# A decoder layer on one core: side-chain transfers issued by POOL, weights alone by SP, convolution taps on shifted ranges

## The chip, the cores and the metric

The kernel runs on 1 core of one Trainium2 chip. Times are microseconds (us) on the device, from the profiler or from a timed execution; single operations are also given in nanoseconds (ns). The engines are PE (TensorE matmul; PEld is its weight load), DVE (VectorE), ACT (ScalarE), POOL (GpSimd) and SP (SyncE). Each executes its own instructions in program order; semaphores order them against each other. A DMA is issued by an instruction on SP or on POOL and moved by the core's 16 DMA engines. The metric is the device time of one execution, given as a median of 3.

## The reference, cut to what matters

One layer for 256 prompt positions and 8 sample positions (264 columns together, `T` in the kernel):

```python
p = x @ w_in                      # [u | v_a | q,k,v | z | beta | a | gate_a | gate_b]
y_a = gelu(u) * (tril(W_s[g]) @ LN(gelu(v_a)) + b_s[g])       # 16 groups, chunks of 128
qkv = silu(causal depthwise conv, width 4, of q,k,v)
q, k = l2norm(q) * 128**-0.5, l2norm(k)
beta, g = sigmoid(.), -exp(A_log) * softplus(a + dt_bias)
S_t = exp(g_t) (I - beta_t k_t k_t^T) S_{t-1} + beta_t k_t v_t^T ;  o_t = S_t^T q_t   # 16 heads
y_b = rmsnorm_head(o) * w_onorm * silu(z)
m = (sigmoid(gate_a) * (y_a W_pa) + sigmoid(gate_b) * (y_b W_pb)) W_o
x1 = LN(ALPHA*x + m);  y = LN(ALPHA*x1 + relu(x1 W_up)^2 W_down)
```

The convolution of the prompt starts from zeros, that of the samples from a state that is passed in. Besides y, the last rows before the convolution and the new recurrent states are returned. All weights are float32; D_MODEL is 2048, d_ff 8192, 16 heads of 128.

## The kernel before

**The stream.** All weights pass through PE once, as 305 blocks of 2048 x 128, each in two halves j of 128 x 1024. A half is loaded into one of 4 `raw` buffers (`dma_w`, line 314), rounded by ACT to `hi` (`hi_w`, line 321), and DVE forms `lo = raw - hi` (`lo_w`, line 327). PE then does 24 matmuls of 264 columns per half (`mms`, lines 379 to 381): hi x xh, hi x xl, lo x xh. The order of the blocks is: beta/a; q, k, v of head groups 0 and 1; va; group 2; gate a; group 3; gate b; u; z; then the projections pa, pb, wo; then up and down. In slot j of the main loop (line 1545) PE's half j is written out, then `hi` of half j+4, `lo` of half j+3, the evacuation of the block that has just ended (`evac_...`), up to one step of each side chain (`step`, line 409), and last the load of half j+7.

**Side chains.** Everything else is written as generators, one step at a time, between the slots: `norm_chain` and `delta_chain`, `final_chain`, `out_chain` of each head group g (names n, d, f, o), `lnv_chain`, `sample_chain`, `ya_chain`, `yb_chain`, `x1_chain`, `state_chain`. A step is written out when the program's own estimate (`clk`, `rdy`, `est`, `dma`) says that its data are there. `require` forces a chain to its end where the stream needs its result: o0 before group 3, lnv before u, ya before pa, yb before pb, x1, state. Side chains repack data through DRAM: a store, then a load in another layout (`repack`, line 785; `d_n` to `N`; `d_t` to `W`; `d_r` to `X`), with broadcast loads among them.

**Issuers.** `dma("y", ...)` issues on SP: the weights, and all loads of the chains and most of their stores. `dma("g", ...)` issues on POOL: the stores `d_sga`, `d_sg`, `d_ya`, `d_z`, `d_mac`, `d_o`, `d_r` and a few small ones. A weight load waits on SP for the `lo` that last read its buffer, and what is issued later on SP waits behind it. POOL's other work is the mask of the decay matrix (line 686), the mask of W_s (`load_ws`, line 1168), the copy of the last columns before the convolution (line 1136), and memsets.

**Steps that are named below.** `delta_chain` loads four broadcast tiles `N` and then a tile of identities, `eye`, on which DVE's triangular solve works (lines 728 to 751). `evac_pa` multiplies a gate tile `mc`, which `load_mc` (line 1194) fetched at the start of the block, by the block's result and stores it to `d_mac`. `load_ws` loads a W_s tile, masks it on POOL and loads a bias tile. `yb_chain` (line 973) builds the input of pb in eight pairs of heads; for the last two it waits for o3, and after them it waits for the sample chain and does the sample columns `zs`. `evac_qkv` (line 1114) copies a block to `cv` behind three zero columns and adds three taps with DVE. The small tiles of all evacuations share one pool `e` of 8 buffers.

Of the kernel before, what the change touches and what calls it, by code (L numbers as in the profile page):

```python
# [89 lines left out]
def hybrid_step(ctx: ExitStack, tc: tile.TileContext, I, O):  # L90
# [61 lines left out]
    clk = {"p": 0.0, "v": 0.0, "a": 0.0, "y": 0.0, "g": 0.0, "d": 0.0}  # L152
# [19 lines left out]
    def dma(q, out, in_, track=True, after=0.0):  # L172
        t = max(clk[q], after, rdy.get(in_.tensor.name, 0.0))
        clk[q] = t + (1050.0 if q == "g" else 60.0)
# [6 lines left out]
        (G_ if q == "g" else nc.sync).dma_start(out=out, in_=in_)  # L181
# [404 lines left out]
    def norm_chain(g):  # L586
# [6 lines left out]
        dma("y", out=sc, in_=I["sconv"][:, :, hs, :, :])  # L593
# [48 lines left out]
        dma("y", out=X, in_=d_r[g, 4:8, :].partition_broadcast(P))  # L642
# [4 lines left out]
        dma("y", out=X, in_=d_r[g, 0:4, :].partition_broadcast(P))  # L647
# [9 lines left out]
    def delta_chain(g):  # L657
# [9 lines left out]
        for c in range(2):  # L667
            dma("y", out=D[c], in_=d_gc[hs, c * P:(c + 1) * P].partition_broadcast(P))
        bN = sm("bN", (P, 32))
        for c in range(2):  # L670
            dma("y", out=bN[64 * c:64 * c + 64, :],
# [37 lines left out]
        for c in range(2):  # L709
            dma("y", out=d_p[g, c], in_=Pm[c])  # L710
# [5 lines left out]
        dma("y", out=nd.rearrange("c h a j i -> (a j) c h i"), in_=dg)  # L716
# [7 lines left out]
        dma("y", out=qd, in_=d_eg[hs, P:2 * P].partition_broadcast(P))  # L724
# [10 lines left out]
        dma("y", out=Tt, in_=I["eye"])  # L735
# [21 lines left out]
        for c in range(2):  # L757
            dma("y", out=tdd[c].rearrange("k p i -> p k i"), in_=Tt[64 * c:64 * c + 64])
# [11 lines left out]
    def load_blocks(g, c):  # L770
        W = dt_("W", (P, 4, P))
        dma("y", out=W[:, 0:3, :], in_=d_p[g, c, 0:96].rearrange("(b j) h i -> (j h) b i", b=3))
        dma("y", out=W[:, 3, :], in_=d_t[g, c].rearrange("k (q h a) i -> (k q h) (a i)", q=4, h=HG))
# [11 lines left out]
    def repack(t, src, to_blocks, dst):  # L785
        if to_blocks:
            dma("y", out=t, in_=src)
        else:
            dma("y", out=t.rearrange("(a i) h v -> (i h) a v", a=4), in_=src)
        yield  # L790
        yield
        if to_blocks:
            dma("y", out=dst, in_=t.rearrange("(a i) h v -> (i h) a v", a=4))
        else:
            dma("y", out=dst, in_=t)
# [104 lines left out]
    def load_state(i, pool, bufs):  # L900
        t = pool.tile([P, SK, P], F32, tag="s", bufs=bufs, name=nm("Ss"))
        dma("y", out=t, in_=I["ssm"][:, SK * i:SK * i + SK, :], track=False)
# [787 lines left out]
```

## Time and profile before

| | us |
|---|---|
| median of 3 executions | 1898.2 (1897.77 to 1898.55) |
| the profiled execution, timed | 1898.92 |
| its span in the profile | 1897.2 |
| PE busy in the span | 1884.2 |
| DVE, ACT, POOL busy | 1281.0, 1038.6, 108.2 |

The granted TensorE clock is full but for the first and the last stretch. A row of the windows view gives the busy time of each engine in a stretch of the span; what PE lacks to the length of the stretch is PE's idle time. Waits are listed by the instruction that waited and by what it waited for. In a timeline the square bracket holds the engine's idle time before the instruction, and what ended it.

### The profile page before, as it was taken

What the parts mean: (1) busy time and instruction counts of PE and PEld (TensorE: products, weight loads), DVE (VectorE), ACT (ScalarE), POOL (GpSimd) and SP (SyncE); (2) the same over time, 40 slices, a digit from 0 to 9 for tenths busy, and PEclk for the clock granted to TensorE, in tenths of its full rate; (3) what the DMA queues carried; (4) which work ended last, traced back from release to release, by engine and by line L of the source; (5) the groups of instructions that cost most, each with busy time, mean ns of one, the idle gap of its engine ahead of it and who ended that gap; (6) DMA issues with size and microseconds to landing.
All of it is one profiled execution on the core that took longest, in us unless ns stands there. A gap on an engine that the chain in (4) does not pass through costs nothing.

```text
span 1897.2 us, 38788 instructions
## 1 busy us (share of the span) xinstructions
PE 1884.2 (99%) x15502; PEld 1880.6 (99%) x15502; DVE 1281.0 (68%) x2208; ACT 1038.6 (55%) x1626; POOL 108.2 (6%) x239
## 2 busy tenths in 40 slices
PE   9999999999999999999999999999999999999998
PEld 9999999999999999999999999999999999999998
DVE  6876768857685779877566778756665644444575
ACT  6777466666665544545444557744654455345552
POOL 1110000011111111001000000000000000000000
PEclk9999999999999999999999999999999999999999
DMA  7656575666667877988877655577777755565552
GB/s 237 192 182 213 178 221 188 211 205 220 200 199 242 258 244 246 300 260 285 259 227 229 203 192 180 174 244 244 239 239 245 235 182 182 182 202 180 177 182 98
DMA packets 167684, 406.72 MB, mean 214 GB/s; under 512 B 31184, under 2 KB 67184, under 8 KB 167360
## 3 DMA queue, kind: packets, MB, share of 16 engines
q1 hardware_dynamic: 161856, 388.38, 64.5%
q0 software_dynamic: 5648, 15.87, 2.2%
q8 instruction: 121, 1.98, 0.4%
q14 instruction: 59, 0.48, 0.1%
HBM read 372.96 MB, written 31.62 MB: 213 GB/s over the span
## 4 chain that ended last, share of the span: by engine, by line
PE 85%; DVE 2%; issue 1%; DMA 1%; ACT 0%; DVEq 0%; POOL 0%; SPq 0%; POOLq 0%; ACTq 0%
PE mm L380 27%; PE mm L379 27%; PE mm L381 27%; PE ax L236 3%; DVE lo L216 1%; PE ax L240 1%; DMA raw<-in_wt 0%; DVE G L216 0%; PE st L236 0%; DVE tmp L216 0%; DVE Y L227 0%; DMA G<-d_y 0%; DVE rr L231 0%; DMA d_ya<-gu 0%; DVE N L216 0%
## 5 line engine op out<-in xcount | busy, mean ns | idle before, releaser
L216 DVE TENSOR_TENSOR lo<-raw,hi 128x1024 fp32r<-128x1024 f32 (+1 forms) x614 | 741.8, 1212 | 347.8 <-PE mm L381 166.6
L197 ACT ACTIVATE hi<-raw 128x1024 fp32r<-128x1024 f32 (+1 forms) x614 | 638.8, 1047 | 376.4 <-PE mm L380 248.4
L379 PE MATMUL mm<-xh,hi 128*128 128x264 f32 x1872 | 538.0, 287 | 0.0
L381 PE MATMUL mm<-xh,lo 128*128 128x264 f32 x1872 | 531.2, 284 | 2.6 <-DVE lo L216 2.5
L380 PE MATMUL mm<-xl,hi 128*128 128x264 f32 x1872 | 532.8, 285 | 0.0
L381 PEld LDWEIGHTS mm<-xh,lo 128*128 128x128 f32 x1872 | 352.1, 188 | 3.7 <-DVE lo L216 3.7
L379 PEld LDWEIGHTS mm<-xh,hi 128*128 128x128 f32 x1872 | 353.0, 189 | 0.1
L380 PEld LDWEIGHTS mm<-xl,hi 128*128 128x128 f32 x1872 | 352.0, 188 | 0.1
L380 PE MATMUL mm<-hl,hi 128*128 128x264 f32 x1024 | 291.6, 285 | 0.0
L381 PE MATMUL mm<-hh,lo 128*128 128x264 f32 x1024 | 290.3, 284 | 0.0
L379 PE MATMUL mm<-hh,hi 128*128 128x264 f32 x1024 | 290.1, 283 | 0.0
L379 PE MATMUL mm<-x1h,hi 128*128 128x264 f32 x784 | 223.5, 285 | 0.0
L381 PE MATMUL mm<-x1h,lo 128*128 128x264 f32 x784 | 222.6, 284 | 0.0
L380 PE MATMUL mm<-x1l,hi 128*128 128x264 f32 x784 | 222.3, 284 | 0.0
L379 PEld LDWEIGHTS mm<-hh,hi 128*128 128x128 f32 x1024 | 192.9, 188 | 0.0
L381 PEld LDWEIGHTS mm<-hh,lo 128*128 128x128 f32 x1024 | 192.8, 188 | 0.0
L380 PEld LDWEIGHTS mm<-hl,hi 128*128 128x128 f32 x1024 | 192.2, 188 | 0.0
L380 PEld LDWEIGHTS mm<-x1l,hi 128*128 128x128 f32 x784 | 147.7, 188 | 0.0
L379 PEld LDWEIGHTS mm<-x1h,hi 128*128 128x128 f32 x784 | 147.4, 188 | 0.0
L381 PEld LDWEIGHTS mm<-x1h,lo 128*128 128x128 f32 x784 | 147.2, 188 | 0.0
L216 DVE TENSOR_TENSOR r<-r,mm 128x264 f32<-128x264 f32 x64 | 27.5, 429 | 104.0 <-PE mm L381 104.0
L227 DVE SCALAR_TENSOR_TENSOR ac<-cv,cols,ac 128x256 f32<-128x256 f32 x144 | 69.5, 483 | 7.8 <-ACT ac L197 4.4
(324 smaller groups left out, 3039.5 us busy)
## 6 DMA issues: line engine op xcount, KB each, us to landing
raw<-in_wt SPq DMA_DIRECT2D x602, 512.0 KB
Ss<-in_ssm SPq DMA_DIRECT2D x64, 256.0 KB
out_ssm_s<-Ss SPq DMA_DIRECT2D x32, 256.0 KB
G<-d_r SPq DMA_DIRECT2D x8, 528.0 KB
raw<-in_wt SPq DMA_DIRECT2D x12, 256.0 KB
d_y<-G SPq DMA_DIRECT2D x12, 256.0 KB
G<-d_y SPq DMA_DIRECT2D x12, 256.0 KB
d_sga<-sg POOLq DMA_DIRECT2D x16, 132.0 KB, 4.1
```

What stands on the lines that cost most here:

```text
L197: S.activation(out=out, in_=in_, func=func, scale=scale)
L216: V.tensor_tensor(out=out, in0=a, in1=b, op=op)
L227: V.scalar_tensor_tensor(out=out, in0=a, scalar=s, in1=b, op0=op0, op1=op1)
L236: PE.matmul(out=out, lhsT=lhsT, rhs=rhs, start=start, stop=stop)
L240: PE.transpose(out, in_, idt)
L379: PE.matmul(out=ps, lhsT=hi[:, kk, :], rhs=xh[:, k, :], start=(k == 0), stop=False)
L380: PE.matmul(out=ps, lhsT=hi[:, kk, :], rhs=xl[:, k, :], start=False, stop=False)
L381: PE.matmul(out=ps, lhsT=lo[:, kk, :], rhs=xh[:, k, :], start=False, stop=(k == 15))
```

## The change

- The queue letter "w" is new and stands for SP; only the weight loads, the first loads of the program and the last stores (`out_y`, `out_ys`) carry it. Every other `dma` call becomes "g", that is POOL.
- The program's estimate of an issue on POOL becomes 600 ns instead of 1050. With it and with the separate queues, the estimated times differ, and so the slots in which side-chain steps are written out.
- `evac_qkv` drops the three zero columns of `cv` and their memset; each tap adds the columns that exist into the columns of `ac` that it reaches.
- `yb_chain` waits for the sample chain and does the sample columns before it waits for o3, instead of after the last pair.

```diff
-    clk = {"p": 0.0, "v": 0.0, "a": 0.0, "y": 0.0, "g": 0.0, "d": 0.0}
+    clk = {"p": 0.0, "v": 0.0, "a": 0.0, "w": 0.0, "g": 0.0, "d": 0.0}
...
     def dma(q, out, in_, track=True, after=0.0):
         t = max(clk[q], after, rdy.get(in_.tensor.name, 0.0))
-        clk[q] = t + (1050.0 if q == "g" else 60.0)
+        clk[q] = t + (60.0 if q == "w" else 600.0)
...
-        (G_ if q == "g" else nc.sync).dma_start(out=out, in_=in_)
+        (nc.sync if q == "w" else G_).dma_start(out=out, in_=in_)
...
-        dma("y", out=raw[j], in_=I["wt"][b - 1, :, 8 * h:8 * h + 8, :], after=lo_end.get(j - RAW, 0.0))
+        dma("w", out=raw[j], in_=I["wt"][b - 1, :, 8 * h:8 * h + 8, :], after=lo_end.get(j - RAW, 0.0))
...
-                dma("y", out=N[s][64 * c:64 * c + 64], in_=ndf.unsqueeze(0).to_broadcast([4, 16, 16, 32]))
+                dma("g", out=N[s][64 * c:64 * c + 64], in_=ndf.unsqueeze(0).to_broadcast([4, 16, 16, 32]))
...
-        dma("y", out=Tt, in_=I["eye"])
+        dma("g", out=Tt, in_=I["eye"])
...
         if to_blocks:
-            dma("y", out=t, in_=src)
+            dma("g", out=t, in_=src)
         else:
-            dma("y", out=t.rearrange("(a i) h v -> (i h) a v", a=4), in_=src)
+            dma("g", out=t.rearrange("(a i) h v -> (i h) a v", a=4), in_=src)
...
                 if i == 6:
+                    yield from wait_for("samp")
+                    zs = qt("zs", (P, KT, TS))
+                    dma("g", out=zs, in_=d_z[:, :, TP:T].rearrange("m p b -> p m b"))
+                    yield
+                    yield
+                    stt(zs, VS, col(C_ON, 0), zs, ALU.mult, ALU.mult)
+                    act(hi[:, :, TP:T], zs, AF.Copy)
+                    yield
+                    tt(lo[:, :, TP:T], zs, hi[:, :, TP:T].bitcast(F32), ALU.subtract)
+                    yield
                     yield from wait_for("o3")
...
-        yield from wait_for("samp")
-        zs = qt("zs", (P, KT, TS))
-        dma("y", out=zs, in_=d_z[:, :, TP:T].rearrange("m p b -> p m b"))
...
-        cv = et("cv", (P, 3 + T))
-        G_.memset(cv[:, 0:3], 0.0)
+        cv = et("cv", (P, T))
         cb = 4 * (16 * s + m)
-        act(cv[:, 3:3 + T], ps, AF.Copy)
+        act(cv, ps, AF.Copy)
...
-            stt(ac, cv[:, t:t + TP], col(cb, t), ac, ALU.mult, ALU.add)
-        G_.tensor_copy(out=tail[:, s, j, :], in_=cv[:, 3 + TP - 3:3 + T])
+            stt(ac[:, 3 - t:TP], cv[:, 0:TP - 3 + t], col(cb, t), ac[:, 3 - t:TP], ALU.mult, ALU.add)
+        G_.tensor_copy(out=tail[:, s, j, :], in_=cv[:, TP - 3:T])
...
         w = et("ws", (P, 2, P))
-        dma("y", out=w, in_=I["wst"][:, 2 * i:2 * i + 2, :])
+        dma("g", out=w, in_=I["wst"][:, 2 * i:2 * i + 2, :])
         G_.affine_select(out=w, in_=w, pattern=[[0, 2], [1, P]], base=0, channel_multiplier=-1,
                          compare_op=ALU.is_ge, fill=0.0)
         bs = et("bs", (P, 2, P))
-        dma("y", out=bs, in_=I["b_s"][2 * i:2 * i + 2, :].partition_broadcast(P))
+        dma("g", out=bs, in_=I["b_s"][2 * i:2 * i + 2, :].partition_broadcast(P))
...
         if kind == "pa":
-            dma("y", out=t[0], in_=d_sga[m])
+            dma("g", out=t[0], in_=d_sga[m])
...
-            dma("y", out=O["y"][c * P:c * P + P, s_], in_=y)
+            dma("w", out=O["y"][c * P:c * P + P, s_], in_=y)
```

## Rows read from the trace of the kernel before

**Rows 1.** The page, part 1: busy time of PE and PEld.

```profile
PE 1884.2 (99%) x15502; PEld 1880.6 (99%) x15502; DVE 1281.0 (68%) x2208; ACT 1038.6 (55%) x1626; POOL 108.2 (6%) x239
```

**Rows 2.** The windows view: stretch, then each engine's busy us (instructions).

```profile
0.00:50.00 50.00, 46.92 (x355) 46.19 (x356) 29.49 (x46) 35.06 (x56) 5.72 (x24) 0.97 0.70 233
200.00:250.00 50.00, 47.45 (x384) 46.57 (x383) 40.57 (x96) 19.62 (x28) 0.54 (x1) 1.00 0.61 192
500.00:550.00 50.00, 48.52 (x405) 48.33 (x404) 35.67 (x77) 29.35 (x69) 5.70 (x13) 1.00 0.60 182
1100.00:1150.00 50.00, 49.67 (x405) 49.33 (x404) 39.14 (x63) 27.92 (x47) 0.00 (x0) 1.00 0.57 183
1850.00:1900.00 50.00, 41.64 (x341) 40.94 (x339) 26.54 (x51) 12.20 (x24) 0.00 (x0) 0.97 0.28 91
```

**Rows 3.** Waits of PE: total us, times, longest us.

```profile
PE mm L381 <- DVE lo L216: 2.5, 3, 1.7
PE ax L236 <- DMA G<-d_y: 1.5, 1, 1.5
```

**Rows 4.** Timeline of DVE around three of its waits: start us, us, instruction, wait.

```profile
206.30 0.43 DVE L216 TENSOR_TENSOR G<-G,bN 128x256 f32<-128x256 f32 x1 [7.17 <-issue]
...
527.31 0.43 DVE L216 TENSOR_TENSOR G<-G,bN 128x256 f32<-128x256 f32 x1 [4.95 <-DMA G<-in_eye]
...
711.62 0.23 DVE L216 TENSOR_TENSOR tmp<-N,G 128x72 f32<-128x72 f32 x1 [3.60 <-DMA d_ya<-gu]
```

**Rows 5.** Timeline of SP before those waits, and around the late load d_y.

```profile
192.87 2.21 SPq L181 DMA_DIRECT2D N<-d_n  x4
...
199.17 0.33 SPq L181 DMA_DIRECT2D G<-in_eye  x1
...
525.17 0.38 SPq L181 DMA_DIRECT2D d_y<-G  x1
...
530.52 0.38 SPq L181 DMA_DIRECT2D G<-d_y  x1
```

**Rows 6.** Waits of SP: the largest group.

```profile
SPq L181 <- DVE lo L216: 976.1, 439, 7.6
```

**Rows 7.** DMA issues by line: issuer, count, KB each, median us to landing.

```profile
Ss<-in_ssm SPq DMA_DIRECT2D x64, 256.0 KB
...
d_sga<-sg POOLq DMA_DIRECT2D x16, 132.0 KB, 4.1
...
d_o<-G POOLq DMA_DIRECT2D x8, 256.0 KB, 5.5
...
zs<-d_z SPq DMA_DIRECT2D x1, 64.0 KB
```

**Rows 8.** The tile d_mac: from issue on POOL to landing.

```profile
DMA to landing us min/median/max: 2.3/4.1/6.7
```

**Rows 9.** Groups of POOL by line: two issues, busy us, mean ns.

```profile
L181 POOL DMA_DIRECT2D d_ya<-gu x16 | 8.8, 548 | 44.3 <-issue 13.3 <-DVE ACC L227 11.6 <-DVE G L216 10.1
...
L181 POOL DMA_DIRECT2D out_tails<-tail x4 | 3.0, 745 | 0.3 <-POOL tail L1136 0.3
```

**Rows 10.** Timelines of DVE, POOL and SP in the pa stage.

```profile
874.16 0.43 DVE L216 TENSOR_TENSOR mc<-mm,mc 128x264 f32<-128x264 f32 x1 [1.69 <-PE mm L381]
...
879.93 0.43 DVE L216 TENSOR_TENSOR mc<-mm,mc 128x264 f32<-128x264 f32 x1 [0.23 <-PE mm L381]
...
880.66 0.54 POOL L181 DMA_DIRECT2D d_mac<-mc  x1 [5.23 <-DVE rr L231]
...
880.17 0.38 SPq L181 DMA_DIRECT2D mc<-d_sga  x1
```

**Rows 11.** The zero columns of the convolution, groups of POOL by line.

```profile
L1128 POOL MEMSET cv<- 128x3 f32 x48 | 4.8, 99 | 0.0
```

**Rows 12.** Timelines of DVE and PE: end of yb, start of pb.

```profile
940.93 0.29 DVE L216 TENSOR_TENSOR ybl<-zs,ybh 128x128 fp32r<-128x128 f32 x1
...
944.82 0.29 PE L379 MATMUL mm<-ybh,hi 128*128 128x264 f32 x1
```

More of the change, by code (lines that the diff above doesn't have):

```diff
@@ L641, in norm_chain @@
         yield
-        dma("y", out=X, in_=d_r[g, 4:8, :].partition_broadcast(P))
+        dma("g", out=X, in_=d_r[g, 4:8, :].partition_broadcast(P))
         yield
@@ L709, in delta_chain @@
         for c in range(2):
-            dma("y", out=d_p[g, c], in_=Pm[c])
+            dma("g", out=d_p[g, c], in_=Pm[c])
             for a in range(4):
@@ L715, in delta_chain @@
         yield
-        dma("y", out=nd.rearrange("c h a j i -> (a j) c h i"), in_=dg)
+        dma("g", out=nd.rearrange("c h a j i -> (a j) c h i"), in_=dg)
         for h in range(HG):
@@ L723, in delta_chain @@
         axf()
-        dma("y", out=qd, in_=d_eg[hs, P:2 * P].partition_broadcast(P))
+        dma("g", out=qd, in_=d_eg[hs, P:2 * P].partition_broadcast(P))
         yield
@@ L792, in repack @@
         if to_blocks:
-            dma("y", out=dst, in_=t.rearrange("(a i) h v -> (i h) a v", a=4))
+            dma("g", out=dst, in_=t.rearrange("(a i) h v -> (i h) a v", a=4))
         else:
-            dma("y", out=dst, in_=t)
+            dma("g", out=dst, in_=t)
         yield
@@ L963, in ya_chain @@
                 t[i] = qt("yld", (P, 2, T))
-                dma("y", out=t[i], in_=d_ya[2 * i:2 * i + 2].rearrange("m p t -> p m t"))
+                dma("g", out=t[i], in_=d_ya[2 * i:2 * i + 2].rearrange("m p t -> p m t"))
             if i >= 2:
@@ L982, in yb_chain @@
                 if i == 6:
+                    yield from wait_for("samp")
[8 more added lines that the diff above has]
+                    yield
                     yield from wait_for("o3")
                 t[i] = (qt("yo", (P, 2, TP)), qt("yz", (P, 2, TP)))
-                dma("y", out=t[i][0], in_=d_o[2 * i:2 * i + 2].rearrange("m p t -> p m t"))
-                dma("y", out=t[i][1], in_=d_z[2 * i:2 * i + 2, :, 0:TP].rearrange("m p t -> p m t"))
+                dma("g", out=t[i][0], in_=d_o[2 * i:2 * i + 2].rearrange("m p t -> p m t"))
+                dma("g", out=t[i][1], in_=d_z[2 * i:2 * i + 2, :, 0:TP].rearrange("m p t -> p m t"))
             if 1 <= i < 9:
@@ L1017, in state_chain @@
             yield "wait"
-            dma("y", out=O["ssm_s"][:, SK * i:SK * i + SK, :], in_=s)
+            dma("g", out=O["ssm_s"][:, SK * i:SK * i + SK, :], in_=s)
             if i + 2 < n:
@@ L1196, in load_mc @@
         if kind == "pa":
-            dma("y", out=t[0], in_=d_sga[m])
+            dma("g", out=t[0], in_=d_sga[m])
         else:
-            dma("y", out=t[0], in_=d_mac[m])
+            dma("g", out=t[0], in_=d_mac[m])
             t.append(et("sgb"))
-            dma("y", out=t[1], in_=d_sg[m])
+            dma("g", out=t[1], in_=d_sg[m])
         ten.setdefault("mc", {})[m] = t
@@ L1223, in evac_wo @@
             nx = et("xr")
-            dma("y", out=nx, in_=I["xt"][:, m + 1, :])
+            dma("g", out=nx, in_=I["xt"][:, m + 1, :])
             ten["xr"][m + 1] = nx
@@ L1447, in load @@
                 sl = slice(*part[1:])
-                dma("y", out=wbr[:, sl, :], in_=I["wba"][:, sl, :])
+                dma("w", out=wbr[:, sl, :], in_=I["wba"][:, sl, :])
             elif part[0] == "x":
                 sl = slice(*part[1:])
-                dma("y", out=xs[:, sl, :], in_=I["xt"][:, sl, :])
+                dma("w", out=xs[:, sl, :], in_=I["xt"][:, sl, :])
             elif part[0] == "w":
@@ L1457, in load @@
                     raw[j] = rawp.tile([P, 8, P], F32, tag="raw", name="raw%d" % j)
-                dma("y", out=raw[j][:, lo:hi, :], in_=I["wt"][b - 1, :, 8 * h + lo:8 * h + hi, :])
+                dma("w", out=raw[j][:, lo:hi, :], in_=I["wt"][b - 1, :, 8 * h + lo:8 * h + hi, :])
             else:
-                dma("y", out=rows2, in_=I["rows2"])
-                dma("y", out=cst, in_=I["cst"])
-                dma("y", out=cols, in_=I["cols"])
+                dma("w", out=rows2, in_=I["rows2"])
+                dma("w", out=cst, in_=I["cst"])
+                dma("w", out=cols, in_=I["cols"])
         def split(part):
@@ L1564, in hybrid_step @@
                     xr = et("xr")
[L1565 removed]
+                    dma("g", out=xr, in_=I["xt"][:, 0, :])
                     ten["xr"] = {0: xr}
```

26 lines of the change are left out of this document (9 added, 17 removed).

## The prediction

> **What bounds the kernel now.** I read the busy times first, then the windows, then the waits of PE, and last the timelines of the engines behind each of those waits. PE is busy for 1884.2 of the 1897.2 us [rows 1], with a granted clock of 1.00 wherever the stream is running [rows 2]. The change leaves every matmul in place, so the most that it can give is PE's idle time, 13.0 us. The windows say where that lies [rows 2]: 50 - 46.92 = 3.08 us in the first stretch, 2.55 in 200 to 250, 1.48 in 500 to 550, 0.33 in 1100 to 1150, and 47.22 - 41.64 = 5.58 in the last (the span ends at 1897.22). These sum to 13.0. The first stretch waits for the first weights and the last for the final layer norm; neither is edited. The one at 1100 is the first layer norm. So 2.55 + 1.48 = 4.03 us can go.
>
> The waits of PE name them [rows 3]: three waits for `lo`, 2.5 us together, and one of 1.5 us for a repacked tile `d_y`. Behind the first lies DVE. It sat idle for 7.17 us before the first operation on the identity tile [rows 4], which SP issued at 199.17 [rows 5]; from issue to use that is 7.13 us. While DVE stood, no `lo` was made and the weights in hand were used up. The same load made DVE wait 4.95 us at 527, and a buffer still held by the store `d_ya` cost it 3.60 us at 711 [rows 4]; neither is followed by a wait of PE for `lo` of its own size in the list [rows 3]. I conclude that PE is covered for about 5 us of one DVE wait, and pays for what lies beyond: 7.17 cost 2.5.
>
> **The change part by part.** My sum is made against the profiled execution, 1898.92 us timed, which is 1.7 above its span and 0.7 above the median of 1898.2. I carry differences over to the median.
>
> *Issues moved from SP to POOL.* The list of DMA issues, from `Ss` with 64 to `zs` with 1 [rows 7], has 313 issues of SP that are neither weights, first loads nor last stores. On POOL an issue takes 0.55 us for a plain tile and 0.75 us for one of many short pieces [rows 9], so 313 cost 170 to 235 us of POOL, whose total becomes some 280 to 340 us of 1897. That much of an engine at 6% lies beside PE; the price is latency, not throughput.
>
> *What SP is rid of.* SP waits 976.1 us for `lo` in 439 waits, 2.2 us each, 7.6 at most [rows 6]; these are weight loads waiting for their buffer, and chain transfers stood behind them. In turn, weight loads no longer stand behind a chain's transfer that waits for its data. `d_y` shows it: its store was issued at 525.17, but its load only at 530.52 [rows 5]. POOL has a head of its line too: stores that wait for an evacuation, the copy of the last columns, the masks. Each holds up a chain by up to a slot, so I take no gain in the length of chains, only in latency.
>
> *The identity tile.* From issue to landing POOL's transfers show 4.1 us at 132 KB and 5.5 at 256 KB [rows 7], 2.3 to 6.7 at the extremes [rows 8]. These are stores; for a load of this kind on POOL the trace has no row, and I take them as bounds. In place of 7.13, the 128 KB tile then arrives in 4.1 to 5.5 us, being nearest to the 132 KB rows, and DVE waits about 4.1 to 5.5 us instead of 7.17. The first of these is covered, the second is 0.5 over the 5 us where 2.2 over cost 2.5. So 2.0 to 2.55 us come back; I take 2.2. With 6.7 it would be 0.6.
>
> *The repacked tile.* On POOL the store lands at 525.17 + 4.1 to 5.5 = 529.3 to 530.7 and the load as much later, 533.4 to 536.2. PE waited until 534.63 or so with a wait of 1.5, that is, it came at about 533.1 [rows 3, 5]. So it would wait 0.3 to 3.1 us instead of 1.5: a gain of 1.2 to a loss of 1.6. I take 0.
>
> *New waits on POOL.* Two loops arise. In `load_ws` the mask waits for the landing of a load that POOL has just issued, and the bias load and the next `d_ya` store stand behind it; a late `d_ya` is what held DVE for 3.60 us at 711 [rows 4]. In the pa stage the store of block m (which waits for DVE's product) now stands ahead of the load of `mc` for block m+1, on which DVE's next product waits. Before, SP issued that load beside the store, at 880.17 against 880.66 [rows 10]. The loop is 0.73 us from product to store [rows 10], 0.54 for the store's issue, then the load's landing of 4.1: 5.4 us against a block's 5.77 us, the distance of two products [rows 10]. At 4.1 us it costs nothing. For both loops together I take 1.0 us, within 0 (the loop fits) and 10 (below).
>
> *The weights' own transfers.* A weight load that shared SP's line now shares only the DMA engines with POOL's transfers, and the bytes stay the same. I take 0, between no gain beyond the 4.03 us above and, at worst, one more stall like the one after 200 us, 2.5.
>
> *Convolution.* 48 memsets of 99 ns [rows 11] go from POOL, and each tap loses one to three of 256 columns on DVE. POOL and DVE are not what PE waits for in those stages: 0.
>
> *Sample columns earlier.* The last write of yb's input ends at 941.2, and PE starts pb at 944.8 [rows 12]: 3.6 us to spare, so no gain today. The move shortens the tail after o3 and is the cover if chains on POOL become later. 0.
>
> Sum: -2.2 + 0 + 1.0 + 0 = -1.2 us, 1898.2 - 1.2 = 1897.0.
>
> One rule speaks against the change as such. The Trainium skill says in "DMA: Bandwidth & Descriptors", section "Issuing engines are not separate DMA queues", that issuing from several engines saves only the sequencer's time to start a transfer. By it the result would be the time before; here the trace agrees with the saving it concedes, since SP's line is held by waits, and differs in that these waits are long [rows 6]. Another, in "SBUF — State Buffer", the box on DVE blocking DMA, has POOL's descriptors wait while DVE holds the shared port, with some 3.1 us in place of 0.62. The trace does not show it at this kernel's DVE operations: issues average 548 ns [rows 9].
>
> **The rivals.**
>
> *All of the idle time goes.* If landings on POOL stay near 4.1 us and neither loop costs anything, both stalls go: 1898.2 - 4.03 = 1894.2. For it: DVE's wait at 200 is half queueing, and SP's weights flow freely. Against it: the repack took two landings in series, and only the shortest of POOL's makes it.
>
> *The loop of the pa stage sets the pace, and the kernel is slower.* If a load lands as late as `d_o` did, 5.5 us [rows 7], the loop is 0.73 + 0.54 + 5.5 = 6.8 us, 1.0 over the block. Over 15 blocks that is 15 us, of which about 5 are covered as above: +10, with the -1.2 some 1907. It begins at a landing of 4.5 us (5.77 - 1.27) and is slower by the bound below from (5 + 1.2 + 3.8)/15 = 0.67 over, at 5.2 us. At 6.7 us [rows 8] it would be 1898.2 + 33 - 5 = 1926, which no median in the rows suggests. For it: POOL's order is fixed, and chain transfers of yb and o3 are issued in the same stretch. Against it: the 132 KB median is 4.1.
>
> *It does not do what it says.* POOL's line takes the place of SP's, chains are held as long as before, the waits of DVE move to other places: 1898.2, with 1896 to 1900.
>
> **How the numbers follow.** A difference under 0.2%, 3.8 us, is about what a measurement of this kernel can't tell from none. My forecast, 1897.0 with 1895 to 1900, gets 0.38; no effect 0.15; all idle time gone 0.25; the loop, or its like in the u stage, 0.22. The first two lie within 0.2%, above 1894.4 and below 1902.0: same 0.53, faster 0.25, slower 0.22. The range reaches down to 1893.4: 4.03 us, the 0.33 at 1100 [rows 2] and the 0.4 by which the lowest of the executions lies under their median are all that I see to win. It reaches up to 1905, between the bound of 1902.0 and the 1907 of the loop, and so cuts off somewhat over half of the slower case.
>
> **What would show it.** Right: no DVE wait over 5 us before an operation on the identity tile; PE idle time in 200 to 250 under 1 us; the loads on POOL landing in 4 to 5 us; the SP waits reduced to `lo`; PE still near 1884 busy. Wrong: DVE waits for `mc` in block after block of the pa stage, with PE idle between 850 and 950; new PE waits for `lo` near 700, behind a late `d_ya`; PE waiting at the start of group 3 or pb for a chain that POOL has made late. The forecast fails as a whole if PE's cadence itself changes, or if the new order of chain steps piles several DVE waits into one stretch.

## The result, and the profile of the changed kernel

| | before | changed kernel |
|---|---|---|
| median | 1898.55 us (5 executions, beside it) | 1917.39 us (5 executions, 1911.79 to 1919.87) |
| span of the profiled execution | 1897.2 us | 1915.6 us |
| PE busy / PE idle in the span | 1884.2 / 13.0 | 1890.2 / 25.4 |
| POOL busy | 108.2 | 297.0 |

The kernel became slower: the ratio of the times is 1.0095, with a 95% interval of 1.0076 to 1.0113. (Ratios and intervals here are those on record; they lie within 0.0006 of the quotient of the medians.) The forecast was 1897.0, in a range of 1893.4 to 1905.0.

I begin where the prediction began, with the busy times (part 1 of the page), which answer to [rows 1].

```profile
PE 1890.2 (99%) x15502; PEld 1884.4 (98%) x15502; DVE 1281.0 (67%) x2208; ACT 1041.3 (54%) x1628; POOL 297.0 (16%) x504
```

The span grew by 18.4 us. PE's idle time grew by 25.4 - 13.0 = 12.4 us and its busy time by 6.0, and these two make up the whole. No matmul was added, so the 6.0 us of busy time must come from slower ones.

The windows view tells where it lies (stretch, length, each engine's busy us with instructions, granted clock, DMA share, GB/s). The rows at 0, 200 and 500 answer to the same stretches in [rows 2], the others are new; the last row is the kernel before in the u stage.

```profile
0.00:50.00 50.00, 47.26 (x370) 46.69 (x371) 30.14 (x46) 35.74 (x57) 5.08 (x18) 1.00 0.72 236
200.00:250.00 50.00, 49.12 (x399) 48.44 (x398) 42.11 (x98) 19.98 (x28) 6.78 (x11) 1.00 0.63 205
500.00:550.00 50.00, 49.93 (x418) 49.73 (x417) 34.83 (x80) 36.09 (x74) 15.06 (x23) 1.00 0.62 185
550.00:600.00 50.00, 47.58 (x390) 46.97 (x389) 35.54 (x69) 29.49 (x43) 9.76 (x16) 1.00 0.68 219
680.00:730.00 50.00, 41.78 (x322) 41.38 (x322) 39.88 (x120) 14.87 (x20) 14.68 (x27) 0.93 0.66 209
860.00:960.00 100.00, 95.97 (x777) 95.20 (x777) 58.21 (x94) 42.58 (x69) 32.66 (x52) 0.98 0.78 247
...
680.00:730.00 50.00, 49.95 (x416) 49.74 (x415) 41.85 (x124) 21.71 (x41) 7.18 (x12) 1.00 0.66 215
```

In the stretches at 200 and 500 PE's idle time fell from 2.55 to 0.88 us and from 1.48 to 0.07, that is by 3.08 us. New idle time is 2.42 us at 550 to 600, 8.22 in the u stage at 680 to 730 (the kernel before had 0.05 there) and 4.03 in the pa stage at 860 to 960, where it had none. The u and pa stages of the changed kernel also show a granted clock below 1.00. Comparing the start of every half in the two traces gives the same picture in time: the changed kernel is mostly 1 to 4 us ahead up to 684 us, loses some 13.5 us between 684 and 727 and some 6.5 us between 889 and 925, and is 18 us behind from there on.

The waits of PE name the causes (waiting operation, what it waited for, total us, times, longest us); they answer to [rows 3].

```profile
PE ax L236 <- DVE G L216: 6.2, 3, 5.5
PE ax L240 <- DVE G L216: 3.2, 2, 2.6
PE ax L236 <- DMA G<-d_y: 2.8, 1, 2.8
...
PE mm L381 <- DVE lo L216: 1.1, 3, 0.5
```

The waits for `lo` went from 2.5 us to 1.1. The new ones are of another kind: `ax` is a matmul of a side chain that stands in PE's own stream, and it waits for that chain's tile itself.

**The u stage.** Three engines tell one story. First POOL, then DVE, then PE (start, duration, operation, and in brackets the idle time before it with what ended it).

```profile
681.55 0.40 POOL L1167 TENSOR_SCALAR_AFFINE_SELECT ws<-ws 128x256 f32<-128x256 f32 x1 [7.49 <-DMA ws<-in_wst]
682.07 0.55 POOL L181 DMA_DIRECT2D bs<-in_b_s  x1
682.62 0.54 POOL L181 DMA_DIRECT2D d_ya<-gu  x1
683.15 0.54 POOL L181 DMA_DIRECT2D Ss<-in_ssm  x1
683.68 0.54 POOL L181 DMA_DIRECT2D G<-in_eye  x1
...
687.01 0.42 DVE L216 TENSOR_TENSOR G<-G,bN 128x256 f32<-128x256 f32 x1 [7.33 <-DMA G<-in_eye]
...
695.32 0.80 PE L236 MATMUL ax<-G,TI 128*128 128x128 f32 x2 [5.46 <-DVE G L216]
...
696.13 0.42 PE L380 MATMUL mm<-xl,hi 128*128 128x264 f32 x1
696.35 0.42 PE L381 MATMUL mm<-xh,lo 128*128 128x264 f32 x1
...
698.33 0.29 PE L381 MATMUL mm<-xh,lo 128*128 128x264 f32 x1
698.45 0.29 PE L379 MATMUL mm<-xh,hi 128*128 128x264 f32 x1
```

POOL had issued the load of a W_s tile and came to the mask of that tile, which waited 7.49 us for it. The identity tile stood four issues behind the mask in the same line. DVE waited 7.33 us for it, and PE waited 5.46 us for the solve that DVE then did. After the wait the matmuls start 0.22 us apart (696.13, 696.35), and from 698.33 on 0.12 apart as everywhere else: in between the clock was granted at the lower of its two levels. The windows put a number on it:

```profile
680.00:700.00 20.00, 14.54 (x109) 14.33 (x109) 12.24 (x38) 4.68 (x6) 5.33 (x10) 0.91 0.47 150
720.00:740.00 20.00, 17.63 (x134) 17.64 (x135) 17.07 (x50) 7.43 (x21) 5.19 (x10) 0.91 0.69 228
...
920.00:940.00 20.00, 20.00 (x154) 19.83 (x154) 12.47 (x16) 8.12 (x11) 7.78 (x13) 0.91 0.81 240
```

A clock of 0.91 over 20 us is at most 1.8 us of full-speed work not done. Three such stretches are 5.4 us. Against them, the first 50 us were granted 1.00 here and 0.97 in the kernel before [rows 2], which is 1.5 us the other way. So the lower clock accounts for some 4 of the 6.0 us by which PE's busy time grew; where the rest lies was not traced. Each lies at or right behind one of PE's three longest waits: 5.46 us ending at 695.32, 2.76 ending at 722.37, 2.56 ending at 919.83.

Behind the second of these three waits POOL's timeline shows the mask again, a few blocks later:

```profile
707.66 0.77 POOL L181 DMA_DIRECT2D d_y<-G  x1
...
713.15 0.48 POOL L1167 TENSOR_SCALAR_AFFINE_SELECT ws<-ws 128x256 f32<-128x256 f32 x1 [4.17 <-DMA ws<-in_wst]
...
715.19 0.54 POOL L181 DMA_DIRECT2D G<-d_y  x1
```

Between the store of `d_y` and the load that reads it back, POOL stood 4.17 us for the next mask. The load was issued 7.5 us after the store (in the kernel before, the same turn of this repack has 5.25 us, 675.74 to 680.99 on SP). PE came to it and waited 2.8 us. The mask is not the whole of this wait: in the run with the mask written late (below), the load still follows its store by 6.8 us, behind a store `d_ya` that waited 3.85 us for DVE, and PE still waits 2.10 us. Nor does the distance alone decide: with SP as issuer in this order it is 9.4 us in the same turn, and PE does not wait.

**The pa stage.** The row of DVE's waits is followed by one turn of the loop on DVE and POOL, which answers to [rows 10], and by the next wait of DVE with what PE did after it.

```profile
DVE mc L216 <- DMA mc<-d_sga: 35.2, 13, 4.6
...
904.57 0.57 POOL L181 DMA_DIRECT2D d_mac<-mc  x1 [4.54 <-DVE mc L216]
905.14 0.55 POOL L181 DMA_DIRECT2D mc<-d_sga  x1
...
910.61 0.43 DVE L216 TENSOR_TENSOR mc<-mm,mc 128x264 f32<-128x264 f32 x1 [4.00 <-issue]
...
911.34 0.55 POOL L181 DMA_DIRECT2D d_mac<-mc  x1 [5.65 <-DVE rr L231]
...
918.74 0.43 DVE L216 TENSOR_TENSOR mc<-mm,mc 128x264 f32<-128x264 f32 x1 [3.50 <-DMA mc<-d_sga]
...
919.83 1.72 PE L240 MATMUL ax<-cst,G 128*128 128x128 f32 x8 [2.56 <-DVE G L216]
```

In 13 of 16 blocks DVE's product waited for its gate tile; the one at 910.61 is put down to "issue", but it too began 5.5 us after the issue of its tile at 905.14. From one store to the next the loop takes 911.34 - 904.57 = 6.77 us, a full us over the 5.77 us of a block [rows 10]. In the next turn two loads of another chain, `yo` and `yz`, stand ahead of the gate tile from 911.87 to 913.31 and put 1.44 us on top; DVE waited 3.50 us.

None of PE's waits in this stage is for these products. Of its 4.03 us of idle time, 3.88 are two waits of chain matmuls, 2.56 and 1.32 us (ending at 919.83 and 899.05), for operations that DVE did behind the products. So the loop did not slow the stream itself; it held DVE, and through DVE a chain for which PE waits directly.

The landing times of POOL's transfers, which the prediction had to guess (last column: median us from issue to landing; beside [rows 7]):

```profile
mc<-d_sga POOLq DMA_DIRECT2D x16, 132.0 KB, 5.3
d_mac<-mc POOLq DMA_DIRECT2D x16, 132.0 KB, 3.4
...
N<-d_n POOLq DMA_DIRECT2D x16, 128.0 KB, 7.3
...
G<-in_eye POOLq DMA_DIRECT2D x4, 128.0 KB, 5.0
```

In the pa stage the load of 132 KB lands 5.3 us after its issue, the store of the same size in the same stage after 3.4. The loads of the other rows land in 5.0 and 7.3. Not every load is that late: `xr`, and `mc` and `sgb` in the pb stage, 132 KB each and issued by POOL, land in 3.9, 4.1 and 4.4 us.

### The profile page after: what moved, and what is told of

Same layout as the page of the kernel before. It is cut to its first block, busy times and chain, and to the rows that moved or that the text cites. A ratio compares the mean times of both kernels' runs of the same rounds, so it can differ in the third digit from the quotient of the medians.

```text
span 1915.6 us, 38802 instructions
## 1 busy us (share of the span) xinstructions
PE 1890.2 (99%) x15502; PEld 1884.4 (98%) x15502; DVE 1281.0 (67%) x2208; ACT 1041.3 (54%) x1628; POOL 297.0 (16%) x504
## 3 DMA queue, kind: packets, MB, share of 16 engines
q0 software_dynamic: 28032, 80.53, 13.5%
## 4 chain that ended last, share of the span: by engine, by line
PE 57%; DMA 2%; DVE 1%; issue 1%; POOL 1%; ACT 0%; DVEq 0%; POOLq 0%
PE mm L379 19%; PE mm L380 19%; PE mm L381 19%; DMA mc<-d_sga 2%; PE ax L236 1%; DMA G<-d_y 1%; DVE Y L227 0%; POOL d_mac L181 0%; PE ax L240 0%; DVE lo L216 0%; DVE mc L216 0%; POOL yo L181 0%; DVE rr L231 0%; DVE r L216 0%; DVE G L216 0%
## 5 line engine op out<-in xcount | busy, mean ns | idle before, releaser
L181 POOL DMA_DIRECT2D out_ssm_s<-Ss x32 | 17.5, 546 | 370.5 <-DVE Ss L227 200.8
```

Of the source, the lines that this page charges most:

```text
L181: (nc.sync if q == "w" else G_).dma_start(out=out, in_=in_)
```

## The experiments

My theory after the traces had two halves. The first is POOL's line: two of its operations wait for transfers that POOL issued itself, and what stands behind them becomes late. The rival is the new order of side-chain steps, which the new estimates bring and which the trace cannot separate from the issuer. So the first runs cross the two.

### The old order with POOL as issuer

The kernel before with its estimates kept, so that every step is written out in the same place (weights, first loads and last stores carry "w", as in the change); only the 313 transfers change their issuer. The traces bear it out: PE, DVE and ACT execute the same sequence as in the kernel before.

```diff
-        t = max(clk[q], after, rdy.get(in_.tensor.name, 0.0))
-        clk[q] = t + (1050.0 if q == "g" else 60.0)
+        c, q = ("y" if q in ("y", "w") else "g"), q
+        t = max(clk[c], after, rdy.get(in_.tensor.name, 0.0))
+        clk[c] = t + (1050.0 if c == "g" else 60.0)
...
-        (G_ if q == "g" else nc.sync).dma_start(out=out, in_=in_)
+        (nc.sync if q == "w" else G_).dma_start(out=out, in_=in_)
```

> The kernel before with its order of instructions, its convolution and its sample columns, but the 313 transfers issued by POOL instead of SP; the estimates that set the order are left as they were. Theory A: the two loops are there with the old order too, so it loses like the changed kernel, 1908 to 1920. Rival B (the new order costs): near the kernel before, 1894 to 1901.

Measured: 1922.15 us, ratio 1.0125 (1.0105 to 1.0145). That is 24 us over the kernel before, more than the whole change costs and 2 us above the range of theory A. The waits of PE and POOL's timeline in the u stage:

```profile
PE ax L237 <- DMA G<-d_y: 10.3, 2, 9.5
PE mm L380 <- DVE mc L217: 3.9, 5, 2.3
...
681.65 0.71 POOL L1169 TENSOR_SCALAR_AFFINE_SELECT ws<-ws 128x256 f32<-128x256 f32 x1 [4.81 <-DMA ws<-in_wst]
...
683.40 0.77 POOL L182 DMA_DIRECT2D d_y<-G  x1
```

The mask again, but this time the store `d_y` stands three issues behind it, and PE waited 9.5 us in one piece for the tile that comes back; its load went out 6.1 us after its store. The two loops are there with either order; who stands behind the mask is what the order decides.

### The new order with SP as issuer

The changed kernel with its estimates and order, in which SP issues what it issued before (one of the calls is shown).

```diff
+        on_sp = q in ("w", "s")
+        q = "w" if q == "w" else "g"
...
-        (nc.sync if q == "w" else G_).dma_start(out=out, in_=in_)
+        (nc.sync if on_sp else G_).dma_start(out=out, in_=in_)
...
-        dma("g", out=Tt, in_=I["eye"])
+        dma("s", out=Tt, in_=I["eye"])
```

> The changed kernel with its order of instructions, its convolution and its sample columns, but the 313 transfers issued by SP as before. Theory A: the loss goes with the issuer, 1894 to 1902. Rival B (the new order costs): above 1908.

Measured: 1906.74 us, ratio 1.0041 (1.0026 to 1.0056), between the two ranges. PE, DVE and ACT execute the same sequence as in the changed kernel. So the order has a price of its own, 8.5 us, with no transfer moved to POOL. PE's waits are 3.7 us for an ACT evacuation `G`, 3.2 for `lo` in four waits and 2.5 for DVE's `G`. The idle time of 2.42 us at 550 to 600 in the changed kernel belongs here: it is made of waits of 0.63 and 1.79 us before two matmuls of the side chains, and with SP as issuer PE waits before the same two, 2.51 and 0.48 us.

The two prices don't add up (24 for the issuer in the old order, 11 in the new one), since each order puts other steps behind the same stalls.

### The loads of the two loops back on SP

The first attempt on the loops took their loads off POOL, in the changed kernel: the W_s tile with its bias, and `mc` of the pa stage, 32 issues.

```diff
-        dma("g", out=w, in_=I["wst"][:, 2 * i:2 * i + 2, :])
+        dma("s", out=w, in_=I["wst"][:, 2 * i:2 * i + 2, :])
...
-        dma("g", out=bs, in_=I["b_s"][2 * i:2 * i + 2, :].partition_broadcast(P))
+        dma("s", out=bs, in_=I["b_s"][2 * i:2 * i + 2, :].partition_broadcast(P))
...
-            dma("g", out=t[0], in_=d_sga[m])
+            dma("s", out=t[0], in_=d_sga[m])
```

> The changed kernel with its order of instructions kept, but the loads of load_ws and the pa loads of mc issued by SP again (32 issues). Theory A (POOL's line: two loops in which POOL waits for, or delays, a load that it issues itself): the 13.5 us lost between 684 and 727 us and the 6.5 us lost in the pa stage go, some 1897 to 1900. Rival B (the new order of the chain steps is what costs, whoever issues): stays above 1910. Rival C (POOL's transfers are slower for all chains alike): under half of the 19 us comes back, above 1908.

Measured: 1911.35 us, ratio 1.0063 (1.0048 to 1.0078), far from the 1897 to 1900 of theory A and in the ranges of both rivals. The trace says why. The stall of the pa stage is gone, since the load of `mc` no longer stands behind a store. The u stage kept its stall:

```profile
684.57 0.52 POOL L1169 TENSOR_SCALAR_AFFINE_SELECT ws<-ws 128x256 f32<-128x256 f32 x1 [6.34 <-DMA ws<-in_wst]
...
691.44 0.43 DVE L218 TENSOR_TENSOR G<-G,bN 128x256 f32<-128x256 f32 x1 [5.37 <-DMA G<-in_eye]
```

The mask still sits in POOL's line and still waits 6.34 us, now for a load that SP issued. What blocks the line is the waiting operation, whoever issued what it waits for. The same run shows that POOL is not what makes these two loads land late: issued by SP, `mc` landed in 5.3 us and `ws` in 4.7 (5.3 and 4.9 on POOL).

### The waits taken out of POOL's line

The cure that follows: leave all transfers on POOL, but write the mask out one block later, when the tile has landed, and the load of the next `mc` ahead of the store of the present one.

```diff
-        G_.affine_select(out=w, in_=w, pattern=[[0, 2], [1, P]], base=0, channel_multiplier=-1,
-                         compare_op=ALU.is_ge, fill=0.0)
...
+    def mask_ws(i):
+        w = ten["ws"][i][0]
+        G_.affine_select(out=w, in_=w, pattern=[[0, 2], [1, P]], base=0, channel_multiplier=-1,
+                         compare_op=ALU.is_ge, fill=0.0)
...
+                    if m % 2 == 0:
+                        mask_ws(m // 2)
...
-                    load_mc(kind, m)
+                    if kind == "pb" or m == 0:
+                        load_mc(kind, m)
...
+                if kind == "pa" and m < 15:
+                    load_mc(kind, m + 1)
```

> The changed kernel with every transfer left on POOL, but the mask of W_s written out one block after its load, and the pa load of mc for block m+1 written out ahead of the store of block m. Theory A (POOL waits in line, not POOL as issuer): most of the 19 us comes back, 1895 to 1903. Rival C (POOL as issuer is slow): above 1908. Rival B (order of the chain steps): above 1910.

Measured: 1904.21 us, ratio 1.0028 (1.0017 to 1.0039), 1.2 us above the range of theory A; 13 us of the 19 are back. DVE's waits for `mc` are left with one of 4.2 us, and POOL's wait for `ws` with one of 0.8:

```profile
DVE mc L216 <- DMA mc<-d_sga: 4.2, 1, 4.2
...
680.00:730.00 50.00, 47.74 (x396) 47.34 (x395) 45.12 (x136) 18.84 (x32) 14.54 (x26) 1.00 0.68 220
```

In the u stage PE's idle time fell from 8.22 to 2.26 us, and the granted clock there is 1.00. The first half of the theory is shown, with its size. Against the new order on SP (1906.74) this is 2.5 us less, and the slowest of its 8 executions, 1905.94, lies just under the fastest of those 4, 1905.96. So rid of its two stalls, POOL as issuer is no worse than SP in this order. The two edits with SP as issuer were not run.

### The late mask alone

Only the first of the two edits, in the changed kernel.

```diff
-        G_.affine_select(out=w, in_=w, pattern=[[0, 2], [1, P]], base=0, channel_multiplier=-1,
-                         compare_op=ALU.is_ge, fill=0.0)
...
+                    if m % 2 == 0:
+                        mask_ws(m // 2)
```

> The changed kernel with the mask of W_s alone written out one block after its load; mc as in the changed kernel. Theory A: the mask's wait on POOL is what the 13.5 us after 684 us come from, and mc's loop is what the 6.5 us of the pa stage come from; so the first goes for the larger part and the second stays: 1906 to 1912, with DVE's wait for the identity tile in the u stage under 5.5 us. Rival (mc's loop carries the most): above 1914.

Measured: 1907.8 us, ratio 1.0049 (1.0034 to 1.0064), as expected. The mask is worth 9.6 us of the 13, the early load of `mc` the other 3.6. DVE's wait for the identity tile in the u stage is 1.82 us, and in the pa stage PE still waits 2.39 us (ending at 911.24), as it should. PE, DVE and ACT execute the same sequence as in the changed kernel, so the 9.6 us are due to the mask's place in POOL's line. The 3.6 us are less clean: with the early load of `mc`, 201 of the 15502 places in PE's sequence hold another matmul.

### Both loops undone in the old order

The old order with POOL as issuer, and the same two edits on top.

> The old order with the 313 transfers on POOL, as one run showed at 1922, with the late mask and the early load of mc added. Theory A (two waits in POOL's line make up most of what POOL costs): 1897 to 1904. Rival C (POOL's longer landings cost everywhere): above 1908.

Measured: 1908.96 us, ratio 1.0054 (1.0039 to 1.0069). That is outside the range of theory A and inside that of rival C. The two loops are worth 13 us here too. What remains, 11 us over the kernel before, is neither the order nor the two loops, and rival C, later landings everywhere, is not excluded in this order. In the changed kernel's order nothing of the kind is left (1904.2 with POOL, 1906.7 with SP). PE's longest wait is 3.7 us for `G<-d_y`, and that is followed up below.

| | before's order | changed kernel's order |
|---|---|---|
| SP issues | 1898.0 | 1906.7 |
| POOL issues | 1922.2 | 1917.4 |
| POOL issues, two waits taken out of its line | 1909.0 | 1904.2 |

### Shorter taps and earlier sample columns, issuers as before

The kernel before with the two small edits, which the prediction put at 0 each.

```diff
-        cv = et("cv", (P, 3 + T))
-        G_.memset(cv[:, 0:3], 0.0)
+        cv = et("cv", (P, T))
...
-            stt(ac, cv[:, t:t + TP], col(cb, t), ac, ALU.mult, ALU.add)
+            stt(ac[:, 3 - t:TP], cv[:, 0:TP - 3 + t], col(cb, t), ac[:, 3 - t:TP], ALU.mult, ALU.add)
...
                 if i == 6:
+                    yield from wait_for("samp")
```

> The kernel before with the new convolution taps and the sample columns ahead of o3 alone; all issuers and estimates of transfers as before. Theory A (issuer plus the order that the new estimates make): these two parts cost nothing, 1896 to 1900. Rival (they shift the order enough to cost): above 1903.

Measured: 1905.83 us, ratio 1.0043 (1.0028 to 1.0058), the rival's range. Two edits that touch neither a bottleneck nor a transfer's issuer cost 8 us. PE waits 4.7 us for DVE's `G` at 511 us, long before the sample columns at 940. So either the taps themselves cost that, or the order does that their estimates bring: the program's estimate of a tap goes by its columns, and one to three columns fewer are 1 to 3 ns.

### The estimate alone, and the taps alone

Two runs tell these apart. The first keeps the old taps and shortens only the estimate.

```diff
-            stt(ac, cv[:, t:t + TP], col(cb, t), ac, ALU.mult, ALU.add)
+            est("v", 130 + 1.04 * (TP - 3 + t), ac, [cv, ac])
+            V.scalar_tensor_tensor(out=ac, in0=cv[:, t:t + TP], scalar=col(cb, t), in1=ac, op0=ALU.mult, op1=ALU.add)
```

> The kernel before with its old taps on 256 columns, but their estimate one to three columns (1 to 3 ns) shorter each, as the new taps have it: only the order of instructions changes. Theory E: 1903 to 1908, with PE waiting directly for a chain's DVE operation for some us near 511. Rival F: 1896 to 1900.

Measured: 1906.35 us, ratio 1.0041 (1.0029 to 1.0053); the 7 executions spread from 1899.42 to 1908.54, the widest spread of all runs.

```profile
PE ax L236 <- DVE G L216: 4.3, 1, 4.3
PE ax L236 <- DMA G<-d_y: 3.5, 1, 3.5
...
500.00:550.00 50.00, 45.67 (x361) 45.46 (x360) 39.80 (x103) 27.60 (x56) 5.99 (x13) 0.93 0.60 172
```

Every operation is as in the kernel before, but for two more table loads on ACT (48 in place of 46); what differs are the slots in which steps are written out. Two chain matmuls now come before their data, 4.3 and 3.5 us too early, and the clock is at 0.93 in the stretch of the first.

The second run has the new taps, with the estimate kept at 256 columns, so that the order stays.

```diff
-            stt(ac, cv[:, t:t + TP], col(cb, t), ac, ALU.mult, ALU.add)
+            est("v", 130 + 1.04 * TP, ac, [cv, ac])
+            V.scalar_tensor_tensor(out=ac[:, 3 - t:TP], in0=cv[:, 0:TP - 3 + t], scalar=col(cb, t),
+                                   in1=ac[:, 3 - t:TP], op0=ALU.mult, op1=ALU.add)
```

> The kernel before with the new convolution taps alone, while the program's estimate of each tap stays that of 256 columns, so that the order of all instructions is the old one; no sample columns moved. Theory E (what the taps cost, 8 us in the run of taps and sample columns, is the order that their new estimates make, not the taps): 1896 to 1900. Rival F (the shifted ranges are slower on the engines): 1903 to 1908, and DVE's taps longer than 485 ns.

Measured: 1899.65 us, ratio 1.0009 (1.0000 to 1.0018). PE, DVE and ACT execute the same sequence as in the kernel before. Together the two runs show that the order costs 8 us and the taps 1.7, at most 3.4 by the interval. They leave nothing that could be seen for the earlier sample columns either, since the run with them (1905.83) is no slower than the run with the estimate alone (1906.35).

### Only the solve's loads on POOL

Back to the step that the prediction valued. The kernel before, its order kept, with the 16 loads of `N` and the four of the identity tile on POOL and nothing else. The letter "p" is issued by POOL but reckoned as SP's, so that the order stays.

```diff
-                dma("y", out=N[s][64 * c:64 * c + 64], in_=ndf.unsqueeze(0).to_broadcast([4, 16, 16, 32]))
+                dma("p", out=N[s][64 * c:64 * c + 64], in_=ndf.unsqueeze(0).to_broadcast([4, 16, 16, 32]))
...
-        dma("y", out=Tt, in_=I["eye"])
+        dma("p", out=Tt, in_=I["eye"])
```

> The kernel before in its old order, with only the 16 loads of N and the 4 of the identity tile issued by POOL. The prediction's step on the identity tile: DVE's wait of 7.17 us falls to 4 to 5.5, PE's three waits for lo after 200 us (2.5 us) fall under 1 us: 1894 to 1897. Rival (POOL's landings are no earlier, 5 to 7 us): 1897 to 1900, no change.

Measured: 1896.14 us, ratio 0.9986 (0.9976 to 0.9995), the only version here that is faster than the kernel before.

```profile
197.49 0.58 POOL L182 DMA_DIRECT2D G<-in_eye  x1 [5.59 <-issue]
201.85 0.42 DVE L217 TENSOR_TENSOR G<-G,bN 128x256 f32<-128x256 f32 x1 [4.93 <-issue]
...
200.00:250.00 50.00, 49.42 (x403) 48.78 (x403) 43.10 (x99) 20.60 (x28) 0.54 (x1) 1.00 0.64 210
500.00:550.00 50.00, 50.00 (x418) 50.00 (x417) 38.65 (x95) 31.79 (x68) 8.42 (x17) 1.00 0.67 203
```

DVE's wait for the identity tile fell from 7.17 to 4.93 us, PE's three waits for `lo` from 2.5 to 1.0. The two stretches that the prediction wanted emptied have 0.58 and 0.00 us of idle time left, of 2.55 and 1.48. Some of that is lost again: 600 to 730 has 1.34 us, where the kernel before had 0.05. What the 16 loads of `N` contribute was not separated.

The Trainium skill says in "DMA: Bandwidth & Descriptors", section "Issuing engines are not separate DMA queues", that spreading issues over engines saves only the sequencer's time. The runs agree that the gain is small, 0.14% at best. What was saved is more than an issue's time, though: from its issue to its use the tile took 4.36 us (197.49 to 201.85) in place of 7.13 [rows 4, 5]. The loss is larger: all 313 transfers in one line with waiting operations cost 1.25% in the old order.

### The repacks on POOL as well

On top of that, the 24 transfers of `d_y` (one of the two pairs of calls is shown), with the mask written late so that it can't hold them.

```diff
         if to_blocks:
-            dma("y", out=t, in_=src)
+            dma("p", out=t, in_=src)
         else:
-            dma("y", out=t.rearrange("(a i) h v -> (i h) a v", a=4), in_=src)
+            dma("p", out=t.rearrange("(a i) h v -> (i h) a v", a=4), in_=src)
```

> As the run with N and the identity tile, with the repacks through d_y issued by POOL as well and the mask of W_s written one block later, so that POOL has no wait of its own in the u stage. If POOL serves these chains without a line in front of it: 1893 to 1897, and PE's wait for d_y at 533 (1.5 us) under 1 us. Rival (two landings of 4.7 and 5.8 us in series are too slow): 1898 to 1904 with PE waiting for d_y.

Measured: 1906.49 us, ratio 1.0046 (1.0032 to 1.006), 10 us more than without the repacks and above both ranges.

```profile
PE ax L237 <- DMA G<-d_y: 5.0, 1, 5.0
...
674.67 0.77 POOL L182 DMA_DIRECT2D d_y<-G  x1
681.67 0.54 POOL L182 DMA_DIRECT2D G<-d_y  x1 [6.24 <-DMA d_y<-G]
```

No mask stood between this store and its load. The load waited 6.24 us for the store to land, 7.0 us from its issue, and PE waited 5.0 us for the load. In the run without the repacks, the same turn has its store at 669.40 and its load at 675.69 on SP, 6.29 us apart, and PE waited 0.65 us. Over all 12 turns the median from store to load is 3.7 us there and 6.7 us here. PE, DVE and ACT execute the same sequence in both. So the repack, two transfers in series for which PE can wait directly, fares badly in POOL's line. That it accounts for the 11 us left over in the old order is likely by its size, but the two kernels differ in more, so I don't call it shown.

### A longer estimate for POOL's transfers

The last run asks whether the order would mend itself if the program reckoned with landings nearer to the measured ones: 3000 ns in place of 1000 for POOL's transfers, on top of the two cures.

```diff
-        f = clk["d"] + (700.0 if out.tensor.name.startswith("raw") else DMA_LAG)
+        f = clk["d"] + (700.0 if out.tensor.name.startswith("raw") else DMA_LAG if q == "w" else 3000.0)
```

> The changed kernel with late mask and early mc, which ran at 1904, and the program's estimate of the lag of a transfer on POOL raised from 1000 to 3000 ns, nearer to the landings that the changed kernel shows (5 to 7 us from issue). Theory D (what is left over, some 6 us, is steps of chains written out before their data land): 1895 to 1901, with PE's direct waits for DVE, ACT and DMA under half. Rival: later steps make chains late for the stream and it stays at 1903 to 1910.

Measured: 1909.1 us, ratio 1.0061 (1.0046 to 1.0076), 5 us worse than with 1000 and in the rival's range. The small waits in the head groups became fewer, but steps were written out later, and yb's chain ended too late: PE waited 6.8 us for `ybh` at 949. A better estimate of one term moved the stall to the end of another chain.

## Why the prediction was wrong, point by point

**The bound, and what could be won: right.** PE's idle time was the right account, and the two stretches named did give 3.08 of the 4.03 us.

**The identity tile: right where the line is free.** The forecast was -2.2 us, from a landing of 4.1 to 5.5. At 200 us it took 5.0 from issue to use (4.4 in the run with these loads alone), DVE waited 5.33 us (4.93), and the idle time at 200 to 250 fell by 1.67 (1.97). That the run with these loads alone gained 1.9 us in the medians is a sum of several stretches and no proof of the one term. In the u stage the same tile was four issues behind a waiting mask, and DVE waited 7.33 us, as long as the 7.17 of the worst turn on SP.

**POOL's load and the weights: right.** POOL became busy for 297 us, forecast as 280 to 340. ACT's waits for the weights' transfers fell from 72.7 to 63.7 us, and PE's for `lo` to 1.1 us. The sign that SP's waits would be for `lo` alone did not come as I put it: 1170 us of them are, but others remain.

**New waits on POOL, the step that failed.** I took 1.0 us for both loops, within 0 to 10. The u stage lost 13.5 us and the pa stage 6.5 in the trace, and taking both waits out gave 13 us back in the medians. Three terms were mis-sized.
- The landing. I priced loads with the medians of stores, 4.1 us, and called it the nearest row. `mc` landed in 5.3. With that, the rival's own sum, (0.73 + 0.54 + 5.3 - 5.77) x 15 = 12 less 5 of cover, gives 7 us, and 6.5 was lost. The rival was right that the loop would not fit into a block, and its chance was too low, for a row of another kind of transfer was taken as evidence against it. That 7 meets 6.5 is luck in part: PE did not lose a share of a block 15 times, it waited twice for a chain and then ran at the lower clock, and undoing the loop gave back 3.6 us in the medians.
- What stands behind the mask. I named the bias load and `d_ya`. The line also held the state tile, the identity tile of the next group and the repack's load, since one line now serves all chains. The prediction asked who waits for the mask, and stopped at the steps that are written beside it in the code.
- The cover. "PE is covered for about 5 us of one DVE wait" came from waits behind which only `lo` was late. Where a chain matmul in PE's stream waits for that chain's result, there is little cover: 7.33 us on DVE became 5.46 on PE, and 3.50 became 2.56.

**The repacked tile.** I took 0, within -1.2 to +1.6, from one turn, the one at 525. That turn did go well: PE's 1.48 us of idle time at 500 to 550 fell to 0.07. But there are 12 turns, and all 24 transfers on POOL cost 10 us when they were added to the run with the solve's loads. In the turn that mattered there the load went out 7.0 us after its store, where I had 4.1 to 5.5, and the wait of PE was 5.0 us where I allowed 3.1.

**The price of a wait.** I valued a microsecond of PE's idle time at one microsecond. In the changed kernel each of the three longest waits has a stretch at the lower clock at or behind its end; the 12.4 us of added idle time came with 6.0 us more of busy time, some 4 of them from the clock.

**The order: left without a price.** Convolution and sample columns were put at 0, and their work does cost nothing that matters. But an estimate that is 1 to 3 ns shorter rewrites the order, and that alone cost 8 us. The prediction names a new order only in its last sentence, as something that would make it fail. The front part had it as a part of the change, and it should have stood in the sum as an edit with an unknown cost, bounded from both sides.

**The rivals.** "All of the idle time goes" was right about the two stretches and wrong about the rest. "It does not do what it says" was wrong in its outcome: POOL's line did take the place of SP's, but the waits grew as they moved. "The loop sets the pace" was the nearest, and its clause "or its like in the u stage" the truth; it was put at 1907, for one of the two. Both came, and the order with them.

What stays open: why one order of steps is 8 us better than another, beyond the waits named; what makes up the 11 us that POOL costs in the old order with its loops undone, the repacks, later landings or other waits in the line; and what the two loops cost in the new order with SP as issuer.

## What to carry to other kernels

When transfers of several chains move to one issuing line, list every operation in that line that waits for a landing, and price what stands behind it in the program's order, not in the code's neighbourhood; a compute operation that waits for its own load should be written out a step later. Move only the transfers that a trace shows to be late on their present issuer (here 20 of 313, for 0.14%), and leave the rest. Where a planner with estimates sets the order, hold the order fixed while testing an edit: 1 to 3 ns of estimate were worth 8 us, four times the best gain found.

## What the runs showed of the hardware that I had not expected

- What a landing costs did not go by size alone. In the pa stage a load of 132 KB landed in 5.3 us (`mc`, from POOL and from SP alike), and a store of 132 KB in 3.4 (`d_mac`); other loads of 132 KB landed in 3.9 to 4.4. Of POOL's loads with 128 KB, the identity tile took 5.0 us and `N`, a broadcast, 7.3.
- Nor did the issuer work one way. The identity tile at 200 us took 7.1 us from issue to use on SP in both orders (199.17 to 206.30 in the kernel before, 198.39 to 205.50 in the new order on SP) and 4.4 to 5.0 on POOL, while a repack's load was issued a median of 3.7 us after its store on SP and 6.7 on POOL, in the same order of steps.
- The Trainium skill gives, in "DMA: Bandwidth & Descriptors", section "Anatomy of one DMA — SWDGE (gpsimd) path", a fit by which 132 KB take some 2.3 us (an estimate from that page). The trace does not agree for this kernel, with its weights in flight: the medians of POOL's transfers of 132 KB lie between 3.4 and 5.3.
- At or behind each of PE's three longest waits in the changed kernel (5.46, 2.76 and 2.56 us) the granted clock was at the lower of its two levels, 1.2 GHz, for a stretch, and matmuls started 0.22 us apart instead of 0.12; each such stretch cost at most 1.8 us by the windows. Not every such wait brought it: with the late mask, the stretch with a wait of 2.10 us was granted 0.97 (680 to 730), that with a wait of 2.39 us 1.00 (860 to 960).
